# A float32 encoder trunk on one core: where seven-product block pairs stand in the down projection, and in which order their parts are converted and multiplied

## The chip, the cores and the metric

One NeuronCore of a Trainium2 chip runs the whole program. The metric is device time in microseconds (us) of one execution; lower is better. Before the change three runs gave 2872.09, 2876.46 and 2876.27 us, a median of 2876.27 us.

## What is computed

The reference is two layers of a bidirectional encoder over 256 tokens of width 2048, in float32. Only the second half of a layer matters here:

```python
        h2 = rms_norm(x, norm2_g[l])
        u = jax.nn.relu(h2 @ w_up[l])
        x = x + (u * u) @ w_down[l]
```

`w_up` is 2048 x 8192 and `w_down` is 8192 x 2048, so the product `(u * u) @ w_down` has 256 rows, an inner size of 8192 and 2048 columns.

## The kernel before

Every large product is made on TensorE with operands split in two: a block of weights of 128 x 2 x 512 elements comes from memory into a `raw` or `rawx` tile (six of them in the second half of a layer), ScalarE writes its rounded part `hi` (tile `whi`, L208 or L226), and VectorE writes the remainder `lo` (tile `wlo`, L209 or L229). A product is then three matmuls of 512 columns (L244 with `hi`, L245 with `lo`, L246 with `hi` again). The program runs through a list of slots; a plain slot is one such block, four products, 12 matmuls. `run_steps` emits slot i on TensorE and, in the middle of it, calls `ahead(i)`, which emits the conversion of slot i + 3 (`convert`), then the loads that have room (`fetch`, L173) and then the loads of block sums (`fetch_sums`, L200 to L203). There are four pairs of `hi` and `lo` tiles, so the conversion of a slot writes into the tiles of the slot four places earlier and waits until TensorE has finished with them. Each engine takes its instructions strictly in the order in which they were emitted. All DMAs but those of L201 go out from SyncE's queue.

The down projection goes in quarters q of 2048 inner elements. In a quarter, columns are taken 1024 at a time as a pair (`add_pair`): two pairs in each of the first three quarters, one in the last, so 7 pairs in a layer and 14 in the run. A pair has 8 places s along the inner size, 256 elements each. At a plain place there are two plain slots (n = 0 and 1). At the three places of `SEVEN` the 2 x 2 blocks are multiplied with 7 products in place of 8 (a Strassen-Winograd scheme): four slots of kinds a, b, c and d with 2, 2, 2 and 1 products.

- Kind a needs the block b0 alone (an ordinary `raw` tile).
- Kinds b and c need sums of weight blocks, held in tile `tsum` (T, four blocks of 128 x 512). A DMA from SyncE loads two blocks into T[1:3] (L200), a DMA from GpSimd adds two more onto them (L201), and VectorE makes T[0] (L227) and T[3] (L228) by adding the two halves of b0.
- Kind d needs the block b22 alone, loaded by L203.

There are two T tiles, used in turn: the sums of the third place of a pair go into the tile of its first place. `fetch_sums` may load sums for at most two places beyond the number that is `used` up, and the load waits until the conversions that read the tile have ended.

Four PSUM banks hold the results of the pair, and four others (tile `psum`: P[1], P[5], P[6], P[7]) gather four of the seven products over the three places. After the last of these, `middle_down` combines them in pieces and adds them to x (L801 an addition to x, L806 a sum, L810 a copy on ScalarE); each piece is run at the beginning of a plain slot. `after_pair` then adds the result banks to x (four instructions, L834). The next unit's accumulators take the banks in turn.

Of the kernel before, what the change touches and what calls it, by code (L numbers as in the profile page):

```python
# [10 lines left out]
F32 = mybir.dt.float32  # L11
FR = mybir.dt.float32r
BF16 = mybir.dt.bfloat16
ACTF = mybir.ActivationFunctionType
ALU = mybir.AluOpType
# [21 lines left out]
AHEAD = 3  # L37
CONVERT_SLOT = 2
RAW_BUFS = 4
SEVEN = (1, 3, 4)  # L40


def shape_constants():
# [28 lines left out]
def encoder_trunk(ctx: ExitStack, tc: tile.TileContext, I, out: bass.AP):  # L72
    nc = tc.nc
# [39 lines left out]
    def start(gen):  # L113
        lanes.append([gen, 0])
# [26 lines left out]
    def add_raw(w, r, c, mlp=False):  # L141
        raws.append((w[r:r + 256, c:c + BLK], mlp))
        return len(raws) - 1
# [6 lines left out]
    def add_pair(w, r0, c0, nkc, act, sums, half, middle, after):  # L150

        u = {"act": act, "after": after, "n": nkc, "form": "pair", "sums": sums, "half": half, "middle": middle}
        for s in range(nkc // 2):
            if s in SEVEN:
                q = {"r": add_raw(w, r0 + 256 * s, c0, True), "w": w[r0 + 256 * s:r0 + 256 * (s + 1), c0:c0 + 2 * BLK],
                     "i": len(summed)}
                summed.append(q)
                for kind in "abcd":
                    slots.append({"u": u, "s": s, "kind": kind, "q": q})
            else:  # L160
                for n in range(2):
                    slots.append({"u": u, "s": s, "kind": "plain", "n": n,
                                  "raw": add_raw(w, r0 + 256 * s, c0 + n * BLK, True)})

    def fetch():

        while free and st["dma"] < len(raws):
            src, mlp = raws[st["dma"]]
            b = free.pop(0)
            if b is not None and not mlp:  # L170
                continue
            t = raw_p.tile([128, 2, BLK], F32, tag="raw", name="raw") if b is None else b
            nc.sync.dma_start(out=t, in_=src.rearrange("(k p) f -> p k f", p=128))  # L173
            raw_t[st["dma"]] = (t, b)
            st["dma"] += 1

    def take(j):
        t, b = raw_t.pop(j)
        return t, lambda: free.append(b)

    def more_room(c):

        T = one.tile([128, 2, 4, BLK], F32, tag="merged", name="tsum")
        c["SU"] = y_p.tile([128, len(SEVEN), 2, 4, 128], FR, tag="yT", name="SU")
        X = y_p.tile([128, 6, BLK], F32, tag="yT", name="rawx")
# [4 lines left out]
    def fetch_sums():  # L190


        while L.get("T") is not None and st["sum"] < min(st["used"] + 2, len(summed)):
            q = summed[st["sum"]]
            if q["i"] >= L["T_end"]:
                return
            T, q["b22"] = L["T"][q["i"] % 2]
            q["T"] = T
            w = q["w"]
            nc.sync.dma_start(out=T[:, 1:3, :], in_=w[0:128, :].rearrange("p (n f) -> p n f", n=2))  # L200
            nc.gpsimd.dma_start(out=T[:, 1:3, :], in_=w[:, BLK:2 * BLK].rearrange("(k p) f -> p k f", p=128),  # L201
                                accum_op=ALU.add)
            nc.sync.dma_start(out=q["b22"], in_=w[128:256, BLK:2 * BLK])  # L203
            st["sum"] += 1

    def lead(hi, lo, src):

        nc.scalar.activation(out=hi, in_=src, func=ACTF.Copy)  # L208
        nc.vector.tensor_tensor(out=lo, in0=src, in1=hi.bitcast(F32), op=ALU.subtract)  # L209

    def convert(upto):
        while st["cv"] <= min(upto, len(slots) - 1):
            sl = slots[st["cv"]]
            kind = sl["kind"]
            hi = hl_p.tile([128, 2, BLK], FR, tag="hi", name="whi")
            lo = hl_p.tile([128, 2, BLK], FR, tag="lo", name="wlo")
            if kind == "plain":
                r, done = take(sl["raw"])
                lead(hi, lo, r)
                done()  # L220
            else:
                q = sl["q"]
                T = q["T"]
                if kind == "a":
                    b0, done = take(q["r"])
                    nc.scalar.activation(out=hi, in_=b0, func=ACTF.Copy)  # L226
                    nc.vector.tensor_tensor(out=T[:, 0, :], in0=T[:, 2, :], in1=b0[:, 0, :], op=ALU.add)  # L227
                    nc.vector.tensor_tensor(out=T[:, 3, :], in0=T[:, 0, :], in1=b0[:, 1, :], op=ALU.add)  # L228
                    nc.vector.tensor_tensor(out=lo, in0=b0, in1=hi.bitcast(F32), op=ALU.subtract)  # L229
                    done()  # L230
                elif kind == "b":
                    lead(hi, lo, T[:, 0:2, :])
                elif kind == "c":
                    lead(hi, lo, T[:, 2:4, :])
                else:
                    lead(hi[:, 1, :], lo[:, 1, :], q["b22"])
                    st["used"] += 1
            hl_t[st["cv"]] = (hi, lo)
            st["cv"] += 1

    def product(o, a, w, kk, first, last):

        hi, lo = w
        nc.tensor.matmul(o, a[0], hi[:, kk, :], start=first, stop=False)  # L244
        nc.tensor.matmul(o, a[0], lo[:, kk, :], start=False, stop=False)  # L245
        nc.tensor.matmul(o, a[1], hi[:, kk, :], start=False, stop=last)  # L246

    def part(a, kc, t):
        ts = slice(128 * t, 128 * t + 128)
        return a[:, kc, 0, ts], a[:, kc, 1, ts]  # L250
# [14 lines left out]
    def run_steps():  # L265
        held = []
        for i, sl in enumerate(slots):
# [16 lines left out]
            if kind != "plain":  # L284
                seven(u, s, kind, a, w, i)
                continue
# [28 lines left out]
    def ahead(i):  # L315
        convert(min(i + AHEAD, 2 * i + 1))
        fetch()
        fetch_sums()
# [10 lines left out]
    def seven(u, s, kind, a, w, i):  # L329

        ps, k0, k1 = u["ps"], 2 * s, 2 * s + 1
        first, last = s == SEVEN[0], s == SEVEN[-1]
        if "P" not in u:
            p = four_banks(1 - u["half"], "psum")
            u["P"] = {1: p[0][0], 6: p[0][1], 5: p[1][0], 7: p[1][1]}
        P, z = u["P"], u["sums"]()[:, SEVEN.index(s)]
        sums = lambda j: (z[:, 0, j - 1, :], z[:, 1, j - 1, :])
        if kind == "a":  # L340
            product(P[1], part(a, k0, 0), w, 0, first, last)
            ahead(i)
            product(ps[0][0], part(a, k1, 0), w, 1, False, False)
        elif kind == "b":
            product(P[6], sums(2), w, 0, first, last)
            ahead(i)
            product(P[5], sums(1), w, 1, first, last)
        elif kind == "c":
            product(P[7], sums(3), w, 0, first, last)
            ahead(i)  # L350
            product(ps[0][1], part(a, k1, 1), w, 1, False, False)
        else:
            ahead(i)
            product(ps[1][0], sums(4), w, 1, False, False)
            if last:
                start(u["middle"](P))

    def feature_banks(u):

# [407 lines left out]
    def after_up(n):  # L767
        def f(ps):
# [14 lines left out]
            def task():  # L783
                for p in range(2):
                    k0 = 4 * n + 2 * p
                    split((U[:, k0:k0 + 2, 0, :], U[:, k0:k0 + 2, 1, :]), E[p])
                    if k0 // 2 in SEVEN:
                        block_sums(c["SU"][:, SEVEN.index(k0 // 2)], E[p])
                    yield
# [3 lines left out]
    def middle_down(n):  # L793

        def pieces(P):
            c = L["c"]
            rs2 = c["rs2"]

            def add(t, nn, u):
                xs = x[:, t, (n + nn) * BLK:(n + nn + 1) * BLK]  # L800
                nc.vector.scalar_tensor_tensor(out=xs, in0=u, scalar=rs2[:, t:t + 1], in1=xs,  # L801
                                               op0=ALU.mult, op1=ALU.add)

            def plus(tag, a, b, op=ALU.add):
                d = w2_p.tile([128, BLK], F32, tag=tag, name="usum")
                nc.vector.tensor_tensor(out=d, in0=a, in1=b, op=op)  # L806
                return d

            u1 = w2_p.tile([128, BLK], F32, tag="V", name="usum")
            nc.scalar.activation(out=u1, in_=P[1], func=ACTF.Copy)  # L810
            yield
            u2 = plus("V", P[6], u1)
            yield
            add(0, 0, u1)
            u4 = plus("L", P[5], u2, ALU.subtract)
            u3 = plus("L", P[7], u2)
            yield
            u5 = plus("eT", P[5], u3, ALU.subtract)
            yield
            add(0, 1, u4)  # L820
            add(1, 0, u3)
            yield
            add(1, 1, u5)
            c["summed"] = True
        return pieces
# [168 lines left out]
    for l in range(DEPTH):  # L994
# [17 lines left out]
        for q in range(4):  # L1012
# [5 lines left out]
            for n in range(NB if q < 3 else 2, NB):  # L1018
                last = l == DEPTH - 1 and q == 3 and n == NB - 1
# [61 lines left out]
```

## Time and profile before

| | |
|---|---|
| runs, median | 2876.27 us (2872.09 to 2876.46) |
| profiled execution, its own time | 2875.01 us |
| its span in the trace | 2873.2 us |
| TensorE busy | 2844.0 us, 99% |
| VectorE busy | 1799.6 us, 63% |
| ScalarE busy | 1427.5 us, 50% |
| mean granted TensorE clock | 0.998 of 2.4 GHz |

PE is TensorE's matmuls, PEld its weight loads, DVE VectorE, ACT ScalarE, POOL GpSimd, SP SyncE; a q after a name is the engine's queue. In a row of the waits stand the engine, the tile and line that waited, after the arrow what ended the wait, then the sum in us, the number of waits and the longest in us. In a row of the timeline stand the start in us, the duration in us, engine, line, operation, output and inputs, shapes and a count, and in brackets how long the engine was idle just before and what ended that. In a row of one line or tile, durations are minimum/median/maximum in ns. Ends of matmuls are modelled by the profiler; starts are recorded.

### The profile page before, as it was taken

The numbers are of one execution on the slowest core, as the hardware profiler recorded it, in microseconds if no ns is written. First come the engines' busy times: TensorE is split into PE (matmuls) and PEld (weight loads), VectorE is DVE, ScalarE is ACT, GpSimd is POOL, SyncE is SP. The second block draws the span as 40 slices with busy tenths as digits, with TensorE's granted clock in tenths as the row PEclk, the third lists the DMA queues.
The fourth block names the chain that finished last, engine by engine and source line by source line (L and its number), as shares of the span: only waits on it lengthen the run. The fifth ranks groups of instructions, "written<-read, shape, count | busy, mean of one in ns | idle before, by whom it ended". The sixth has DMA issues, their size and how long they took to land.

```text
span 2873.2 us, 36216 instructions
## 1 busy us (share of the span) xinstructions
PE 2844.0 (99%) x13816; PEld 2367.1 (82%) x13816; DVE 1799.6 (63%) x2241; ACT 1427.5 (50%) x1818; POOL 155.3 (5%) x146
## 2 busy tenths in 40 slices
PE   8999999999999999999999999999999999999998
PEld 7888888888888888888788888888888888888887
DVE  5465555555677786877644654545556877868775
ACT  5455445444554554555544554454454555545454
POOL 1000001010000010000000000011000000000001
PEclk9999999999999999999999999999999999999999
DMA  7656566555768586775465566655557775857754
GB/s 233 199 152 192 195 177 172 189 185 183 229 220 247 177 256 205 224 218 191 166 213 183 155 195 195 183 162 188 189 185 236 222 223 190 271 178 227 236 179 161
DMA packets 287903, 573.06 MB, mean 199 GB/s; under 512 B 18196, under 2 KB 18382, under 8 KB 287600
## 3 DMA queue, kind: packets, MB, share of 16 engines
q1 hardware_dynamic: 272016, 534.64, 56.1%
q0 software_dynamic: 15376, 35.30, 7.7%
q8 instruction: 108, 1.77, 0.2%
q10 hardware_dynamic: 336, 0.80, 0.1%
q14 instruction: 67, 0.55, 0.1%
HBM read 568.54 MB, written 2.13 MB: 199 GB/s over the span
## 4 chain that ended last, share of the span: by engine, by line
PE 92%; DMA 4%; DVE 2%; ACT 1%; issue 1%; SPq 0%; POOLq 0%; POOL 0%; DVEq 0%
PE acc L244 20%; PE acc L246 20%; PE acc L245 20%; PE acc L262 17%; PE acc L263 8%; DMA tsum<-in_w_down_dram 4%; PE psum L245 1%; PE psum L246 1%; DVE wlo L209 1%; PE psum L244 1%; PE ob L572 1%; PE scb L540 0%; PE xt L419 0%; PE sca L598 0%; ACT whi L208 0%
## 5 line engine op out<-in xcount | busy, mean ns | idle before, releaser
L209 DVE TENSOR_TENSOR wlo<-raw,whi 128x1024 fp32r<-128x1024 f32 x786 | 971.2, 1241 | 707.6 <-ACT whi L208 702.1
L208 ACT ACTIVATE whi<-raw 128x1024 fp32r<-128x1024 f32 x786 | 826.9, 1057 | 727.1 <-PE acc L246 504.7
L262 PE MATMUL acc<-H,whi 128*128 128x512 f32 x2048 | 724.7, 399 | 0.0
L263 PE MATMUL acc<-H,wlo 128*128 128x256 f32 x2048 | 575.2, 281 | 0.0
L244 PE MATMUL acc<-whi,H 128*128 128x512 f32 x1408 | 564.9, 401 | 0.0
L246 PE MATMUL acc<-whi,H 128*128 128x512 f32 x1408 | 550.2, 391 | 0.0
L245 PE MATMUL acc<-wlo,H 128*128 128x512 f32 x1408 | 549.6, 390 | 0.4 <-DVE wlo L209 0.4
L262 PEld LDWEIGHTS acc<-H,whi 128*128 128x128 f32 x2048 | 384.8, 188 | 96.2 <-DVE x L741 0.6
L263 PEld LDWEIGHTS acc<-H,wlo 128*128 128x128 f32 x2048 | 386.9, 189 | 0.3
L244 PEld LDWEIGHTS acc<-whi,H 128*128 128x128 f32 x1408 | 265.1, 188 | 58.8 <-issue 8.1
L246 PEld LDWEIGHTS acc<-whi,H 128*128 128x128 f32 x1408 | 264.7, 188 | 56.9
L245 PEld LDWEIGHTS acc<-wlo,H 128*128 128x128 f32 x1408 | 265.2, 188 | 52.7 <-DVE wlo L209 1.4
L244 PE MATMUL acc<-whi,U 128*128 128x512 f32 x772 | 301.5, 391 | 2.2 <-ACT junk L429 2.2
L245 PE MATMUL acc<-wlo,U 128*128 128x512 f32 x772 | 300.7, 390 | 0.0
L246 PE MATMUL acc<-whi,U 128*128 128x512 f32 x772 | 300.7, 390 | 0.0
L209 DVE TENSOR_TENSOR wlo<-rawx,whi 128x1024 fp32r<-128x1024 f32 (+1 forms) x164 | 177.2, 1086 | 99.2 <-ACT whi L208 96.7
L208 ACT ACTIVATE whi<-rawx 128x1024 fp32r<-128x1024 f32 (+1 forms) x164 | 155.1, 947 | 155.7 <-PE acc L246 79.6
L244 PEld LDWEIGHTS acc<-whi,U 128*128 128x128 f32 x772 | 144.9, 188 | 33.1 <-ACT junk L429 3.0
L246 PEld LDWEIGHTS acc<-whi,U 128*128 128x128 f32 x772 | 145.0, 188 | 30.4
L245 PEld LDWEIGHTS acc<-wlo,U 128*128 128x128 f32 x772 | 145.1, 188 | 29.6
L208 ACT ACTIVATE whi<-tsum 128x1024 fp32r<-128x1024 f32 x84 | 87.9, 1056 | 59.8 <-DVE tsum L227 25.0
L201 POOL DMA_DIRECT2D tsum<-in_w_down_dram x42 | 50.6, 1206 | 1198.0 <-DMA tsum<-in_w_down_dram 820.0
(193 smaller groups left out, 2763.1 us busy)
## 6 DMA issues: line engine op xcount, KB each, us to landing
raw<-in_w_in_dram SPq DMA_DIRECT2D x352, 512.0 KB, 4.1
raw<-in_w_up_dram SPq DMA_DIRECT2D x180, 512.0 KB, 4.3
raw<-in_w_down_dram SPq DMA_DIRECT2D x154, 512.0 KB, 4.7
rawx<-in_w_up_dram SPq DMA_DIRECT2D x76, 512.0 KB, 4.5
raw<-in_w_out_dram SPq DMA_DIRECT2D x64, 512.0 KB, 4.2
rawx<-in_w_down_dram SPq DMA_DIRECT2D x60, 512.0 KB, 5.2
tsum<-in_w_down_dram SPq DMA_DIRECT2D x42, 512.0 KB, 5.6
tsum<-in_w_down_dram POOLq DMA_DIRECT2D x42, 512.0 KB, 9.5
```

The source lines that it names most:

```text
L201: nc.gpsimd.dma_start(out=T[:, 1:3, :], in_=w[:, BLK:2 * BLK].rearrange("(k p) f -> p k f", p=128), accum_op=ALU.add)
L208: nc.scalar.activation(out=hi, in_=src, func=ACTF.Copy)
L209: nc.vector.tensor_tensor(out=lo, in0=src, in1=hi.bitcast(F32), op=ALU.subtract)
L244: nc.tensor.matmul(o, a[0], hi[:, kk, :], start=first, stop=False)
L245: nc.tensor.matmul(o, a[0], lo[:, kk, :], start=False, stop=False)
L246: nc.tensor.matmul(o, a[1], hi[:, kk, :], start=False, stop=last)
L262: nc.tensor.matmul(ps[j], hi[:, kk, fs], a[:, kc, :, :], start=first, stop=False)
L263: nc.tensor.matmul(ps[j][:, S:2 * S], lo[:, kk, fs], a[:, kc, 0, :], start=False, stop=last)
L572: nc.tensor.matmul(o[:, g, :], eT[:, 2 * g + kc, :], c["vb"][:, kc, col:col + 64], start=kc == 0, stop=kc == 1)
```

## The change

`SEVEN` goes from places 1, 3 and 4 to 1, 3 and 5 (counted from 0), so that two plain slots stand between all places with 7 products. The order of kinds goes from a, b, c, d to a, d, b, c, in the list of slots and so in conversion and multiplication. The two additions that make T[0] and T[3] move from the conversion of a to that of b, behind the conversions of a and d; b0's tile is given back there. The copy of P[1] (first piece of `middle_down`) is emitted in the last slot a of the pair, and the other pieces are packed into four, since four plain slots are left behind the last place.

```diff
-SEVEN = (1, 3, 4)
+SEVEN = (1, 3, 5)
...
-                for kind in "abcd":
+                for kind in "adbc":
...
                 if kind == "a":
                     b0, done = take(q["r"])
-                    nc.scalar.activation(out=hi, in_=b0, func=ACTF.Copy)
+                    lead(hi, lo, b0)
+                    q["b0"], q["done"] = b0, done
+                elif kind == "d":
+                    lead(hi[:, 1, :], lo[:, 1, :], q["b22"])
+                elif kind == "b":
+                    b0 = q["b0"]
                     nc.vector.tensor_tensor(out=T[:, 0, :], in0=T[:, 2, :], in1=b0[:, 0, :], op=ALU.add)
                     nc.vector.tensor_tensor(out=T[:, 3, :], in0=T[:, 0, :], in1=b0[:, 1, :], op=ALU.add)
-                    nc.vector.tensor_tensor(out=lo, in0=b0, in1=hi.bitcast(F32), op=ALU.subtract)
-                    done()
-                elif kind == "b":
+                    q["done"]()
                     lead(hi, lo, T[:, 0:2, :])
-                elif kind == "c":
+                else:
                     lead(hi, lo, T[:, 2:4, :])
-                else:
-                    lead(hi[:, 1, :], lo[:, 1, :], q["b22"])
                     st["used"] += 1
...
             product(ps[0][0], part(a, k1, 0), w, 1, False, False)
+            if last:
+                u["rest"] = u["middle"](P)
+                next(u["rest"])
+        elif kind == "d":
+            ahead(i)
+            product(ps[1][0], sums(4), w, 1, False, False)
...
             if last:
-                start(u["middle"](P))
+                start(u["rest"])
...
             u2 = plus("V", P[6], u1)
-            yield
             add(0, 0, u1)
             u4 = plus("L", P[5], u2, ALU.subtract)
+            yield
+            add(0, 1, u4)
             u3 = plus("L", P[7], u2)
             yield
             u5 = plus("eT", P[5], u3, ALU.subtract)
-            yield
-            add(0, 1, u4)
             add(1, 0, u3)
             yield
             add(1, 1, u5)
```

VectorE's order in the first pair of the run, from the plain place 2 to the last seven-product place, before (`tsum` is T; a `wlo` of 128x1024 from `raw` at L229 is that of kind a, the 128x512 one is that of kind d):

```order
L209 TENSOR_TENSOR wlo<-raw,whi 128x1024 x2
L227 TENSOR_TENSOR tsum<-tsum,raw 128x512
L228 TENSOR_TENSOR tsum<-tsum,raw 128x512
L229 TENSOR_TENSOR wlo<-raw,whi 128x1024
L209 TENSOR_TENSOR wlo<-tsum,whi 128x1024 x2
L209 TENSOR_TENSOR wlo<-rawx,whi 128x512
L227 TENSOR_TENSOR tsum<-tsum,raw 128x512
L228 TENSOR_TENSOR tsum<-tsum,raw 128x512
L229 TENSOR_TENSOR wlo<-raw,whi 128x1024
L209 TENSOR_TENSOR wlo<-tsum,whi 128x1024 x2
L209 TENSOR_TENSOR wlo<-rawx,whi 128x512
```

The same stretch in the changed kernel, where the two additions are L232 and L233:

```order
L209 TENSOR_TENSOR wlo<-raw,whi 128x1024 x3
L209 TENSOR_TENSOR wlo<-rawx,whi 128x512
L232 TENSOR_TENSOR tsum<-tsum,raw 128x512
L233 TENSOR_TENSOR tsum<-tsum,raw 128x512
L209 TENSOR_TENSOR wlo<-tsum,whi 128x1024 x2
L209 TENSOR_TENSOR wlo<-raw,whi 128x1024
L209 TENSOR_TENSOR wlo<-rawx,whi 128x1024 x2
L209 TENSOR_TENSOR wlo<-rawx,whi 128x512
L232 TENSOR_TENSOR tsum<-tsum,rawx 128x512
L233 TENSOR_TENSOR tsum<-tsum,rawx 128x512
L209 TENSOR_TENSOR wlo<-tsum,whi 128x1024 x2
```

Nothing that reads T stands ahead of the remainders of a and d any more, and the conversions of two plain slots lie between the second and the third place.

VectorE's order at the end of the first pair, before, from the first sum of P banks to the last addition of `middle_down` (behind it come the two additions to T and the remainder of the next pair's kind a, and then the four rows of `after_pair`):

```order
L806 TENSOR_TENSOR usum<-psum,usum 128x512
L209 TENSOR_TENSOR wlo<-raw,whi 128x1024
L801 SCALAR_TENSOR_TENSOR x<-usum,rs_5619,x 128x512
L806 TENSOR_TENSOR usum<-psum,usum 128x512 x2
L209 TENSOR_TENSOR wlo<-raw,whi 128x1024
L806 TENSOR_TENSOR usum<-psum,usum 128x512
L209 TENSOR_TENSOR wlo<-rawx,whi 128x1024
L801 SCALAR_TENSOR_TENSOR x<-usum,rs_5619,x 128x512 x2
L209 TENSOR_TENSOR wlo<-rawx,whi 128x1024
L801 SCALAR_TENSOR_TENSOR x<-usum,rs_5619,x 128x512
```

And in the changed kernel, where they are L810 and L805 (behind the last row, the remainder of the next pair's kind a, come the four rows of `after_pair`, L837):

```order
L810 TENSOR_TENSOR usum<-psum,usum 128x512
L805 SCALAR_TENSOR_TENSOR x<-usum,rs_5619,x 128x512
L810 TENSOR_TENSOR usum<-psum,usum 128x512
L209 TENSOR_TENSOR wlo<-raw,whi 128x1024
L805 SCALAR_TENSOR_TENSOR x<-usum,rs_5619,x 128x512
L810 TENSOR_TENSOR usum<-psum,usum 128x512
L209 TENSOR_TENSOR wlo<-rawx,whi 128x1024
L810 TENSOR_TENSOR usum<-psum,usum 128x512
L805 SCALAR_TENSOR_TENSOR x<-usum,rs_5619,x 128x512
L209 TENSOR_TENSOR wlo<-rawx,whi 128x1024
L805 SCALAR_TENSOR_TENSOR x<-usum,rs_5619,x 128x512
L209 TENSOR_TENSOR wlo<-raw,whi 128x1024
```

The same eight instructions lie between fewer conversions: three of them stand ahead of the first.

## Rows read from the trace of the kernel before

**Rows 1.** The page: span, busy time of two engines, granted clock by slice.
```profile
span 2873.2 us, 36216 instructions
PE 2844.0 (99%) x13816; PEld 2367.1 (82%) x13816; DVE 1799.6 (63%) x2241; ACT 1427.5 (50%) x1818; POOL 155.3 (5%) x146
...
PEclk9999999999999999999999999999999999999999
```

**Rows 2.** The waits, of PE alone: two of its five rows.
```profile
PE psum L245 <- DVE wlo L229: 10.5, 9, 1.8
...
PE acc L244 <- ACT junk L429: 2.2, 2, 1.1
```

**Rows 3.** Line 227, the first addition to T: what its engine waited for.
```profile
  DMA tsum<-in_w_down_dram: 18.8, 9
```

**Rows 4.** Timeline of PE where the longest stall stands (third place of a pair).
```profile
1369.90 0.39 PE L244 MATMUL psum<-whi,U 128*128 128x512 f32 x1
1372.10 0.50 PE L245 MATMUL psum<-wlo,U 128*128 128x512 f32 x1 [1.81 <-DVE wlo L229]
1372.44 0.42 PE L246 MATMUL psum<-whi,U 128*128 128x512 f32 x1
```

**Rows 5.** Timeline of the same pair: its first place on PE, load of T.
```profile
1354.94 0.39 PE L244 MATMUL psum<-whi,U 128*128 128x512 f32 x1
...
1355.75 0.34 SPq L200 DMA_DIRECT2D tsum<-in_w_down_dram  x1
...
1359.42 1.21 POOL L201 DMA_DIRECT2D tsum<-in_w_down_dram  x1 [110.53 <-DVE wlo L209]
```

**Rows 6.** Timeline of DVE at that pair's third place: additions to T, remainder of a.
```profile
1369.49 0.69 DVE L227 TENSOR_TENSOR tsum<-tsum,raw 128x512 f32<-128x512 f32 x1 [2.74 <-DMA tsum<-in_w_down_dram]
1370.22 0.69 DVE L228 TENSOR_TENSOR tsum<-tsum,raw 128x512 f32<-128x512 f32 x1
1370.83 1.22 DVE L229 TENSOR_TENSOR wlo<-raw,whi 128x1024 fp32r<-128x1024 f32 x1
1371.96 1.22 DVE L209 TENSOR_TENSOR wlo<-tsum,whi 128x1024 fp32r<-128x1024 f32 x1
```

**Rows 7.** Timelines of DVE and ACT at that pair's first place, beside the up projection's end.
```profile
1351.81 0.69 DVE L379 TENSOR_TENSOR U<-u,U 128x512 fp32r<-128x512 f32 x1
1352.76 1.23 DVE L209 TENSOR_TENSOR wlo<-tsum,whi 128x1024 fp32r<-128x1024 f32 x1 [0.26 <-ACT whi L208]
...
1354.51 1.22 DVE L209 TENSOR_TENSOR wlo<-tsum,whi 128x1024 fp32r<-128x1024 f32 x1
...
1351.68 1.04 ACT L208 ACTIVATE whi<-tsum 128x1024 fp32r<-128x1024 f32 x1
1355.20 0.63 ACT L208 ACTIVATE whi<-rawx 128x512 fp32r<-128x512 f32 x1 [1.00 <-PE acc L246]
```

**Rows 8.** Timelines where that layer's last pair ends: DVE, then PE.
```profile
1393.27 1.23 DVE L209 TENSOR_TENSOR wlo<-raw,whi 128x1024 fp32r<-128x1024 f32 x1 [0.83 <-ACT whi L208]
1394.41 2.72 DVE L834 SCALAR_TENSOR_TENSOR x<-acc,rs,x 128x512 f32<-128x512 f32 x4
...
1391.30 0.39 PE L244 MATMUL acc<-whi,U 128*128 128x512 f32 x1
...
1394.47 0.39 PE L246 MATMUL acc<-whi,U 128*128 128x512 f32 x1
1395.96 0.47 PE L244 MATMUL acc<-whi,U 128*128 128x512 f32 x1 [1.10 <-ACT junk L429]
```

**Rows 9.** Lines 801 and 806: the instructions that combine P banks.
```profile
L801 DVE SCALAR_TENSOR_TENSOR x<-usum,rs,x x56: 742/745/747, 856.1 to 2816.5; 128x512 f32<-128x512 f32 x56
...
L806 DVE TENSOR_TENSOR usum<-psum,usum x56: 678/681/687, 854.1 to 2811.3; 128x512 f32<-128x512 f32 x56
```

**Rows 10.** Lines 201 and 200: T's two DMAs, from issue to landing.
```profile
DMA to landing us min/median/max: 7.6/9.5/12.8
...
DMA to landing us min/median/max: 3.1/5.6/8.3
```

More of the change, by code (lines that the diff above doesn't have):

```diff
@@ L347, in seven @@
             product(P[5], sums(1), w, 1, first, last)
-        elif kind == "c":
+        else:
             product(P[7], sums(3), w, 0, first, last)
@@ L351, in seven @@
             product(ps[0][1], part(a, k1, 1), w, 1, False, False)
-        else:
-            ahead(i)
-            product(ps[1][0], sums(4), w, 1, False, False)
             if last:
-                start(u["middle"](P))
+                start(u["rest"])
     def feature_banks(u):
```

## The prediction

> **What bounds the kernel now.** I read the page first. TensorE is busy for 2844.0 of 2873.2 us and its granted clock stands at 9 tenths or more in all 40 slices [rows 1]. The change neither adds nor removes a matmul, so it can only win or lose time in which TensorE stands still, and that is little: 29 us by the page. The waits of PE say how much of it the change can reach. The largest of five entries lies in the stage that the diff touches: PE waits for the remainder of a kind-a block (L229), 9 times, 10.5 us, the longest 1.8 us [rows 2]. The next question is what holds that remainder. Line 227, an addition to T that stands ahead of it on VectorE, waited for the DMA of `tsum` 9 times, 18.8 us [rows 3]: as many waits as TensorE has, so the root is not VectorE's load but a late transfer.
>
> The timeline of the worst case shows the whole chain. At the third seven-product place TensorE issues its first matmul at 1369.90, and the second, which needs `lo`, only at 1372.10 [rows 4]. VectorE had waited 2.74 us for T and began the additions at 1369.49; `lo` began at 1370.83 and ended at 1372.05 [rows 6]. T is the tile that the first place of this pair used. That place began on TensorE at 1354.94 (call it A); the load of T left at 1355.75, when kind c's remainder, begun at 1354.51, had been read out of it [rows 5, 7]. Load, accumulating DMA and arrival took 1369.49 - 1355.75 = 13.74 us [rows 5, 6].
>
> **What a stall costs.** In steady state matmuls start 0.226 us apart: 1391.30 to 1394.47 is 14 steps [rows 8]. The wait in brackets counts from a modelled end 0.39 us after the start, so each of the 9 waits hides 0.39 - 0.23 = 0.16 us more. The matmul behind the stall is followed after 0.34 us rather than 0.23, another 0.11 [rows 4]. Together 10.5 + 9 x 0.16 + 9 x 0.11 = **12.9 us** that the change could give back.
>
> The Trainium skill, "Perfetto Trace Analysis", Tensor Engine Instruction, says that the profiler estimates a TensorE instruction's end and does not observe it. By that rule busy and idle sums are not to be trusted and starts are; by the idle sum alone the gain would be 10.5 us.
>
> **The change, part by part.**
>
> *T's deadline.* Before, the third place begins at A + 14.96 [rows 4, 5], its second matmul 0.23 later, and additions and remainder take 1372.05 - 1369.49 = 2.56 us plus 0.05 to reach TensorE [rows 4, 6]. So the first addition had to start at A + 12.58, or 1367.52. It started 1.97 us later, which is the stall: 1372.10 - 1369.90 - 0.23 = 1.97. Now two plain slots more lie in between, 24 x 0.226 = 5.43 us, and T is needed for b, which comes after a and d, nine matmuls or 2.04 us. b's second matmul is then at A + 14.96 + 5.43 + 2.04 + 0.23 = A + 22.66. Behind the first addition stand 0.69 of its own, the rounding on ScalarE, 1.04, the remainder, 1.22 [rows 6, 7], and three hand-overs, for which I take 0.3. The first addition must start by A + 19.4.
>
> *T's arrival.* The load leaves when c's remainder is done, and c is now last of four. At the first place of a pair that follows the up projection VectorE still carries that projection's own splits. From its split at 1351.81 [rows 7] the new order gives: d's remainder from 1352.45 (0.69), the second split, the two additions from about 1353.7 to 1355.05, b's rounding from 1354.6 behind the first addition, b's remainder 1355.7 to 1356.9, c's to 1358.05. So L200 leaves at about A + 3.1, 2.3 us later than now. With the same 13.74 us T is there at A + 16.8, **2.6 us ahead of the deadline**. At the pairs that follow a pair the figure is about the same, since there c's rounding waits for the slot in front of the place to end, as kind d's does now (1355.20, A + 0.26) [rows 7], and rounding and remainder follow. All 9 stalls should go: -12.9 us.
>
> *Additions moved from a to b.* They leave a's path and enter b's. b's remainder, at 1356.9, is needed at A + 2.04 + 0.23 = 1357.21, c's, at 1358.05, at 1358.57. Both are covered, by 0.3 and 0.5 us. I cost this at nothing; if VectorE is that much slower, each of the 14 first places pays the excess. b0's tile is given back some 3 us later; it is one of six tiles, and no wait of PE leads to a plain block of w_down, so nothing is charged.
>
> *Kind d earlier.* Same instructions, same queues; its rounding waits for no T. Nothing.
>
> *`middle_down` in four slots.* VectorE has to do four sums (0.68), four additions to x (0.745) [rows 9] and four remainders (1.13 apart [rows 6]) in four plain slots: 10.2 us of work in 48 x 0.226 = 10.87 us. Before, it had six slots. Where the next unit takes other banks, or the remainders run three slots ahead, this is covered. It is not at the last pair of each layer, where the next unit needs the very banks that `after_pair` reads: there TensorE stands 1395.96 - 1394.47 - 0.23 = 1.26 us already [rows 8]. In the old order VectorE was idle 0.83 us ahead of the last remainder [rows 8]; in the new one the remainder ahead of the sums ends about 1.65 us into the four slots (it waits for kind b's tiles), and 10.0 to 10.2 us of work follow, so `after_pair` begins some 11.7 us after 1383.83, the start of the four slots, at 1395.5 where it was 1394.41. That is 1.1 us later, twice: **+2.2 us**, between 0 and 2.6. The copy of P[1] in the last slot a sits on ScalarE between two roundings that both wait for TensorE; nothing.
>
> *Sum.* -12.9 + 2.2 = -10.7 us. The profiled execution took 2875.01 us, so 2864.3; it lies 1.26 us under the median of the runs shown, so I expect **2865.5 us**, 0.37% less.
>
> **The rivals.**
>
> 1. *VectorE becomes the bound at the seams.* From the last place of a pair through the next pair's first, VectorE has hardly a gap: the four slots above, then four `after_pair` additions of 0.7 (2.72 in all [rows 8]), two plain remainders and the work of the first place. My margins for b and c there are 0.3 to 0.6 us. Against it: VectorE is busy for only 1799.6 us of the span [rows 1], and before the change it caught up every time. If each of the 14 pairs pays 0.5 us, 7 of the 10.7 us are lost: 2872.5, no measurable change.
>
> 2. *The load of T gets longer, and the stall comes back larger: slower.* L200 leaves 2.3 us later and so nearer to the loads of plain blocks, and lies on more of the path. Its landing has been as late as 8.3 us and that of L201 12.8 [rows 10]; with 1.2 us to issue [rows 5] that is 22.3 us. From A + 3.1 that would be A + 25.4, a stall of 6.0 us. It decides from 16.3 us on (the deadline less 3.1). At 20 us every pair stalls 3.7 us, 14 x 3.7 = 52 us: 2876.3 + 52 - 10.7, about 2917 us. Against it: where T was waited for it took 13.74 us at its worst stall, and the slow landings are also counted where nobody waited.
>
> The Trainium skill, "DMA: Bandwidth & Descriptors", Issuing engines are not separate DMA queues, says that DMAs of all engines run on the same 16 DMA engines and interleave. It is by that rule that a load moved beside others would be slowed; what it adds here no page states, and the bounds are the landings above.
>
> 3. *The stalls do not come from T alone.* If two plain slots between the places were not what was missing, because kind a's remainder is late for want of its tile, the 9 stalls stay and only the 2.2 us are paid: 2878 us. Against it: the remainder began 0.6 us after the second addition in each step of the timeline, and the additions only when T came [rows 6].
>
> **How the numbers follow.** A run-to-run spread of 2872.09 to 2876.46 us makes 0.2%, or 5.8 us, about the least that a measurement can tell. I give the forecast 0.76, rival 1 0.13, rival 2 0.05, rival 3 0.06. The forecast's own bounds are 2863.4 (nothing paid at the seams) to 2867 (2.6 us paid and 1 us of small stalls). The range runs from 2861, with 2 us of spread below, to 2871, which takes in rival 1 up to 0.4 us a pair. Faster by over 0.2% (under 2870.5): 0.76 + 0.07 of rival 1, 0.83. Within 0.2%: the rest of rival 1 and rival 3, 0.12. Slower: rival 2, 0.05.
>
> **What would show it.** Right: PE has no wait for a remainder of a or b in the pairs; the first addition to T waits for no DMA; T's load leaves some 3 us behind the start of the first place and takes 12 to 14 us; the third place lies 20.4 us behind the first; the gap at the end of a layer's last pair grows from 1.5 to about 2.6 us between starts. Wrong: a wait of PE for b's or c's remainder at first places (rival 1), a wait for `tsum` in line 232 (rival 2), or the same 9 waits at kind a (rival 3).

## The result and the profile after

The changed kernel takes 2861.56 us (median of four runs, 2861.08 to 2862.78); the kernel before, run beside it, 2876.36 us (2872.09 to 2879.57). The ratio is 0.995 with a 95% interval of 0.9933 to 0.9967: 14.8 us less by the medians, where 10.8 were forecast. The profiled executions stand closer together: 2875.01 before, 2862.78 after, 12.2 us less. Part of the difference between the two figures is which run was profiled: before, it lay 1.35 us under its median; after, it was the longest of the four.

The page of the changed kernel, against [rows 1]:

```profile
span 2861.0 us, 36205 instructions
PE 2840.8 (99%) x13816; PEld 2367.1 (83%) x13816; DVE 1792.9 (63%) x2241; ACT 1423.2 (50%) x1818; POOL 155.3 (5%) x146
...
PEclk9999999999999999999999999999999999999999
```

Each of the five counts is the same as before; the 11 fewer instructions in the total are in none of them. The waits of PE, all three that are left, against [rows 2]:

```profile
PE xt L423 <- DMA x<-in_x_dram: 4.1, 2, 2.6
PE acc L245 <- ACT junk L433: 3.9, 2, 2.4
PE v1t L897 <- DMA ident<-in_c_ident_dram: 2.9, 1, 2.9
```

The nine waits for kind a's remainder, 10.5 us, are gone, and no wait for a remainder has come in their place. The two waits at the ends of the layers' last pairs have grown from 2.2 to 3.9 us together.

The pair whose third place stalled longest [rows 4 to 7], in the changed kernel: timelines of PE, SyncE's queue, GpSimd and VectorE. The line numbers of the matmuls are one higher (L245 to L247), the first addition to T is L232.

```profile
1349.95 0.39 PE L245 MATMUL psum<-whi,U 128*128 128x512 f32 x1
...
1352.98 0.34 SPq L200 DMA_DIRECT2D tsum<-in_w_down_dram  x1
...
1358.02 1.21 POOL L201 DMA_DIRECT2D tsum<-in_w_down_dram  x1 [109.07 <-DVE tsum L232]
...
1366.87 0.68 DVE L232 TENSOR_TENSOR tsum<-tsum,rawx 128x512 f32<-128x512 f32 x1
...
1370.35 0.39 PE L245 MATMUL psum<-whi,U 128*128 128x512 f32 x1
1370.58 0.39 PE L246 MATMUL psum<-wlo,U 128*128 128x512 f32 x1
```

With A = 1349.95 the load of T leaves at A + 3.03 (it was A + 0.81), the first addition starts at A + 16.92 without having waited for a DMA (the bracket of L201 names VectorE, but L201 left 0.56 us behind the landing of L200, as it did before the change), and the third place begins at A + 20.40. Its second matmul follows 0.23 us behind the first, where it was 2.20 [rows 4].

What got worse stands at the ends of the layers' last pairs. Timelines of the changed kernel, first the first layer's end (against [rows 8]), VectorE and then PE, then the second's, PE and then ScalarE:

```profile
1384.99 1.21 DVE L209 TENSOR_TENSOR wlo<-raw,whi 128x1024 fp32r<-128x1024 f32 x1
1386.12 2.71 DVE L837 SCALAR_TENSOR_TENSOR x<-acc,rs,x 128x512 f32<-128x512 f32 x4
...
1385.78 0.39 PE L247 MATMUL acc<-whi,U 128*128 128x512 f32 x1
1387.67 0.47 PE L245 MATMUL acc<-whi,U 128*128 128x512 f32 x1 [1.50 <-ACT junk L433]
...
2804.11 0.39 PE L247 MATMUL acc<-whi,U 128*128 128x512 f32 x1
2806.91 0.47 PE L245 MATMUL acc<-whi,U 128*128 128x512 f32 x1 [2.42 <-ACT junk L433]
...
2798.94 1.06 ACT L208 ACTIVATE whi<-raw 128x1024 fp32r<-128x1024 f32 x1 [4.22 <-DMA raw<-in_w_down_dram]
```

The gap between starts was 1.49 us [rows 8]; it is now 1.89 and 2.80 us. At the first layer's end VectorE works through the packed sums without a gap and reaches `after_pair` 0.34 us behind the start of the pair's last matmul; before, it was there 0.06 us ahead. At the second layer's end ScalarE had in addition waited 4.22 us for a plain block (2.04 at the first), and VectorE fell back further.

### The profile page after: what moved, and what is told of

Its sections match the earlier page's. It is cut to its first block, busy times and chain, and to the rows that moved or that the text cites. A ratio compares the mean times of both kernels' runs of the same rounds, so it can differ in the third digit from the quotient of the medians.

```text
span 2861.0 us, 36205 instructions
## 1 busy us (share of the span) xinstructions
PE 2840.8 (99%) x13816; PEld 2367.1 (83%) x13816; DVE 1792.9 (63%) x2241; ACT 1423.2 (50%) x1818; POOL 155.3 (5%) x146
## 4 chain that ended last, share of the span: by engine, by line
PE 98%; DVE 1%; issue 0%; ACT 0%; DMA 0%; POOLq 0%; DVEq 0%; POOL 0%; SPq 0%; ACTq 0%
PE acc L245 22%; PE acc L247 21%; PE acc L246 21%; PE acc L263 17%; PE acc L264 8%; PE psum L247 1%; PE psum L245 1%; PE psum L246 1%; PE ob L576 1%; PE scb L544 0%; PE xt L423 0%; PE sca L602 0%; PE oa L636 0%; PE qkt L493 0%; DVE wlo L209 0%
## 5 line engine op out<-in xcount | busy, mean ns | idle before, releaser
L209 DVE TENSOR_TENSOR wlo<-raw,whi 128x1024 fp32r<-128x1024 f32 x814 | 1001.6, 1239 | 686.5 <-ACT whi L208 683.3
L208 ACT ACTIVATE whi<-raw 128x1024 fp32r<-128x1024 f32 x814 | 852.7, 1057 | 700.5 <-PE acc L247 478.6
L245 PE MATMUL acc<-whi,H 128*128 128x512 f32 x1408 | 564.6, 401 | 0.0
L247 PE MATMUL acc<-whi,H 128*128 128x512 f32 x1408 | 549.9, 391 | 0.0
L245 PEld LDWEIGHTS acc<-whi,H 128*128 128x128 f32 x1408 | 264.9, 188 | 58.9 <-issue 8.1
L247 PEld LDWEIGHTS acc<-whi,H 128*128 128x128 f32 x1408 | 264.6, 188 | 56.5
L245 PE MATMUL acc<-whi,U 128*128 128x512 f32 x772 | 301.9, 391 | 3.9 <-ACT junk L433 3.9
L247 PE MATMUL acc<-whi,U 128*128 128x512 f32 x772 | 301.0, 390 | 0.0
L209 DVE TENSOR_TENSOR wlo<-rawx,whi 128x1024 fp32r<-128x1024 f32 (+1 forms) x178 | 192.1, 1094 | 70.8 <-ACT whi L208 69.9
L208 ACT ACTIVATE whi<-rawx 128x1024 fp32r<-128x1024 f32 (+1 forms) x178 | 168.9, 956 | 122.8 <-PE acc L263 70.0
L245 PEld LDWEIGHTS acc<-whi,U 128*128 128x128 f32 x772 | 145.2, 188 | 34.7 <-ACT junk L433 4.7
L247 PEld LDWEIGHTS acc<-whi,U 128*128 128x128 f32 x772 | 145.3, 188 | 30.4
L209 DVE TENSOR_TENSOR wlo<-tsum,whi 128x1024 fp32r<-128x1024 f32 x84 | 102.2, 1224 | 68.8 <-ACT whi L208 68.8
```

## Experiments

Every run is told beside the kernel before, run on the same chip in the same job: 2872.84 us (nine runs, 2869.41 to 2879.24) for the first four, 2873.70 us (seven runs, 2870.48 to 2876.92) for the last four.

**Place 5 alone.** The change, with the old order and the additions back in a:

```diff
-                for kind in "adbc":
+                for kind in "abcd":
...
                 if kind == "a":
                     b0, done = take(q["r"])
-                    lead(hi, lo, b0)
+                    nc.scalar.activation(out=hi, in_=b0, func=ACTF.Copy)
...
+                    nc.vector.tensor_tensor(out=lo, in0=b0, in1=hi.bitcast(F32), op=ALU.subtract)
```

> The changed kernel with its place 5 and its four pieces of middle_down, but with the old order of kinds (a, b, c, d) and the two additions to T back in the conversion of a. Theory (the stalls came from a late T, and the two plain slots more between second and third place are what mends it): the first addition must start by A + 18.0 (A the start of the first place), T's load leaves at about A + 0.8 as before and T is there at about A + 14.6, so no wait for tsum and no wait of PE for a remainder of kind a; 2861 to 2864 us, like the change. Rival (the order of kinds and the additions behind a are needed too, since VectorE's additions ahead of a's remainder hold it up): PE waits for that remainder at places 3 and 5, some 0.7 us a time, 2868 us or more.

2864.01 us, ratio 0.9968 (0.9955 to 0.9981). No wait for a remainder in the pairs and none for `tsum` on VectorE: the theory's reading holds, and the spacing of places, with the four pieces that go with it, removes the stalls without the new order. It is 2.4 us above the changed kernel's median; the two ratios' intervals overlap, but the trace shows what the order adds. Timeline of PE in this run, at the last place of a pair, from the end of kind a to kind b:

```profile
851.95 0.39 PE L246 MATMUL acc<-whi,U 128*128 128x512 f32 x1
852.35 0.50 PE L244 MATMUL psum<-whi,SU 128*128 128x512 f32 x1
852.68 0.40 PE L245 MATMUL psum<-wlo,SU 128*128 128x512 f32 x1
...
851.70 0.60 ACT L813 ACTIVATE usum<-psum 128x512 f32<-128x512 f32 x1
```

b's first matmul comes 0.40 us behind a's last and the next after 0.33, where 0.23 is the rule: 0.27 us lost, just as ScalarE's copy of P[1] ends (852.30). The same step stands at all 14 last places, 0.28 us each by the starts, 4.0 us together. b writes P[6], which lies in the same tile as P[1].

**The order alone.** Places 1, 3, 4 and six pieces as before, kinds a, d, b, c, additions in b:

```diff
-                for kind in "abcd":
+                for kind in "adbc":
```

> The kernel before with places 1, 3 and 4 and middle_down in six pieces as they were, but with the order a, d, b, c and the additions in the conversion of b. Theory: T's load leaves 2.3 us later than before, since c is now last, and the deadline moves only from A + 12.6 to about A + 14.0, since b comes after a and d; so every third place stalls, by 1.7 to 2.8 us behind the up projection (8 pairs) and up to 0.6 us elsewhere (6 pairs): the stalls cost 18 to 26 us where they cost 13, and stalls over about 2 us bring TensorE's clock down to 1.2 GHz for some matmuls on top, 1 to 2 us each. 2882 to 2900 us. Rival (the additions ahead of a's remainder were the fault): the stalls go and the time is 2863 us.

2887.21 us, ratio 1.004 (1.0025 to 1.0055): slower, as the deadline said. The waits of PE in this run, the first two:

```profile
PE psum L246 <- DVE wlo L209: 10.3, 14, 0.8
PE psum L245 <- ACT whi L208: 7.3, 10, 1.3
```

All 14 pairs now wait for b's parts at the third place, 17.6 us by the modelled ends where 10.5 were lost before; by the starts it is about 24 us where it was 12.9, inside the 18 to 26 expected. The clock falls behind the two longest stalls, which lost 2.5 us each (to 1068.74 and 1204.87). It does not fall behind two that lost 2.4 us (to 2636.47 and 2813.38) and one that lost 2.0, so "over about 2 us" is no limit that this run bears out. The stretch behind one of the two, busy time of each engine, then granted clock, DMA share and GB/s:

```profile
1204.00:1209.00 5.00, 4.24 (x12) 3.27 (x12) 5.00 (x5) 3.94 (x5) 0.64 (x1) 0.66 0.84 195
```

So the half of the change that looks like the cleverer one is a loss by itself: it makes T later by more than it moves the deadline.

**No accumulating DMA.** The kernel before without this instruction:

```diff
-            nc.gpsimd.dma_start(out=T[:, 1:3, :], in_=w[:, BLK:2 * BLK].rearrange("(k p) f -> p k f", p=128),
-                                accum_op=ALU.add)
```

> The kernel before without the 42 accumulating DMAs from GpSimd: T then holds two blocks of weights in place of their sums, so the products of kinds b and c are made from the wrong sums; everything else is as before. Theory: T is ready some 9 us earlier, the nine waits for tsum go and with them TensorE's nine waits for a's remainder: 2861 to 2864 us. Rival (the third place came too soon behind the second for VectorE's and ScalarE's own work): the waits stay, 2873 to 2877 us.

2857.37 us, ratio 0.9939 (0.9924 to 0.9954). VectorE's line for the first addition shows no wait for a DMA at all, and PE's waits for a's remainder are gone, with places, order and pieces as before. So it was T's transfer that held them. This run also takes 42 transfers of 512 KB off the DMA engines and so does not tell T's lateness from the traffic; place 5 alone does, where all DMAs stay. That the time lies 3.6 us under the lower end expected fits the layers' ends, which the old six pieces leave at 1.49 us between starts (1384.39 to 1385.88 in its timeline) where the change pays 1.89 and 2.80 and a fall of the clock behind the second.

**Result banks emptied earlier.** The change, with the first two additions of `after_pair` moved behind the slot that finishes those banks:

```diff
+            if u["form"] == "pair" and s == n // 2 - 1 and sl["n"] == 0:
+                pair_out(ps, 2 * u["half"], 0)
             if final:
...
-                for t in range(2):
-                    nc.vector.scalar_tensor_tensor(out=x[:, t, cols], in0=ps[nn][t], scalar=c["rs2"][:, t:t + 1],
-                                                   in1=x[:, t, cols], op0=ALU.mult, op1=ALU.add)
+                if nn == 1:
+                    pair_out(ps, n, 1)
```

> The changed kernel, with the two additions of after_pair that empty the first two result banks emitted one slot earlier, behind the slot that finishes these banks. Theory (the gaps at the last pair of each layer, 1.9 and 2.8 us between starts in the changed kernel, are VectorE's backlog ahead of these two additions): both gaps fall below 1 us and the clock no longer falls behind the second, 2861.6 - 1.2 - 2.0 - 1.4, about 2857 us. Rival (the gap is set by the last product or by the conversions that wait for raw blocks): 2860 to 2862 us.

2857.80 us, ratio 0.994 (0.9925 to 0.9955). The gap at the first layer's end is gone (another of 1.38 us, in front of transposes of x some 6 us later, gives most of that back: the transposes wait for VectorE); the one at the second is down to 0.77 us, and the clock does not fall behind it. Timeline of PE in this run:

```profile
2804.20 0.39 PE L247 MATMUL acc<-whi,U 128*128 128x512 f32 x1
2804.97 0.47 PE L245 MATMUL acc<-whi,U 128*128 128x512 f32 x1 [0.38 <-ACT junk L435]
```

**final_g loaded later.** The change, with one engine's name exchanged:

```diff
-                nc.gpsimd.dma_start(out=fin["g"], in_=I["final_g"].rearrange("(o d) -> o d", o=1).to_broadcast([128, D]))
+                nc.sync.dma_start(out=fin["g"], in_=I["final_g"].rearrange("(o d) -> o d", o=1).to_broadcast([128, D]))
```

> The changed kernel with the load of final_g (1 MB) issued from SyncE's queue, where it stands behind the last pair's loads, in place of GpSimd's, where it leaves as soon as T is free. Theory (at the last pair of the run that load goes out 1 us ahead of a plain block's and delays it, ScalarE waits 4.2 us for the block, VectorE falls back, and the gap there is 2.8 us where it is 1.9 at the other layer's last pair, long enough for the clock to fall): no wait of ScalarE for raw of w_down over 1 us, a gap of about 1.9 us at both, no matmuls at 1.2 GHz behind it; 2861.6 - 0.9 - 1.4, about 2859.3 us. Rival (the gap there is VectorE's backlog alone): 2861 to 2862 us.

2858.10 us, ratio 0.9944 (0.9929 to 0.9959). ScalarE's longest wait for a block of w_down falls from 4.2 to 1.8 us, not under 1 as I had put it; the gap at the run's last pair falls to that of the other layer, and the clock behind it stays up. Timeline of PE and the stretch behind, in this run:

```profile
2801.62 0.39 PE L247 MATMUL acc<-whi,U 128*128 128x512 f32 x1
2803.51 0.47 PE L245 MATMUL acc<-whi,U 128*128 128x512 f32 x1 [1.50 <-ACT junk L433]
...
2803.00:2809.00 6.00, 5.49 (x24) 4.58 (x25) 3.97 (x5) 4.53 (x10) 0.00 (x0) 1.00 0.84 287
```

**Both.** The two edits together:

```diff
+                pair_out(ps, 2 * u["half"], 0)
...
-                nc.gpsimd.dma_start(out=fin["g"], in_=I["final_g"].rearrange("(o d) -> o d", o=1).to_broadcast([128, D]))
+                nc.sync.dma_start(out=fin["g"], in_=I["final_g"].rearrange("(o d) -> o d", o=1).to_broadcast([128, D]))
```

> The changed kernel with both edits: the first two result banks emptied one slot earlier, and final_g loaded from SyncE's queue. Theory: the gap behind the last pair of the run falls from 0.8 to 0.4 us or less between starts; 2857 to 2858 us, 4 us under the change. Rival (the load of final_g, now later, delays plain blocks of the last two units): 2859 us or more.

2857.02 us (2854.63 to 2859.55), ratio 0.9939 (0.9925 to 0.9954). The wait behind the last pair is gone from PE's list. This is the fastest kernel here by its median, 16.7 us under the kernel before; against the two single edits the difference is inside the spread. Its four runs stand in two groups, 2854.63 and 2854.86 against 2859.17 and 2859.55, with none near the median; the trace is of the shortest and does not show what sets them apart.

**Additions back in a.** The change, with the two additions where they were:

```diff
-                    lead(hi, lo, b0)
-                    q["b0"], q["done"] = b0, done
+                    nc.scalar.activation(out=hi, in_=b0, func=ACTF.Copy)
+                    nc.vector.tensor_tensor(out=T[:, 0, :], in0=T[:, 2, :], in1=b0[:, 0, :], op=ALU.add)
+                    nc.vector.tensor_tensor(out=T[:, 3, :], in0=T[:, 0, :], in1=b0[:, 1, :], op=ALU.add)
+                    nc.vector.tensor_tensor(out=lo, in0=b0, in1=hi.bitcast(F32), op=ALU.subtract)
+                    done()
```

> The changed kernel with the two additions to T back in the conversion of a; places 1, 3, 5 and the order a, d, b, c stay. Theory (with two plain slots between the places T has time to spare, so where the additions stand does not matter): T leaves at about A + 3 and is there at A + 16.8 at the latest, 1.2 us ahead of this order's deadline of A + 18.0; 2861 to 2863 us. Rival (the additions had to move behind a and d): waits of PE for a's remainder, 2866 us or more.

2861.73 us, ratio 0.9955 (0.994 to 0.997), and no wait of PE for a remainder. Where the additions stand makes no difference once the places are two plain slots apart.

**Old order, copy later.** The run with place 5 alone, with the copy of P[1] put behind the last place:

```diff
-            if last:
-                u["rest"] = u["middle"](P)
-                next(u["rest"])
...
-                start(u["rest"])
+                start(u["middle"](P))
...
             nc.scalar.activation(out=u1, in_=P[1], func=ACTF.Copy)
-            yield
```

> The run with place 5 and the old order a, b, c, d, but the copy of P[1] goes back from the last slot a to the first piece behind the place. Theory (what that run lost against the change, some 2.4 us, is a hold of 0.3 us a pair and more at the last b: its product goes into a bank of the tile that ScalarE is just copying P[1] from, and kind d in between hides that copy in the change's order): the step at the last b goes, 2860 to 2862 us, unless the gaps at the layers' ends grow. Rival (the step comes from the roundings of b, late in the order a, b): it stays, 2864 us.

2861.68 us, ratio 0.9954 (0.9938 to 0.9971). The step at the last b is gone at all 14 places; the profiled executions, 2866.12 with the step and 2862.45 without, differ by 3.7 us. Timeline of PE, the same place as above:

```profile
851.27 0.39 PE L246 MATMUL acc<-whi,U 128*128 128x512 f32 x1
851.49 0.39 PE L244 MATMUL psum<-whi,SU 128*128 128x512 f32 x1
851.72 0.39 PE L245 MATMUL psum<-wlo,SU 128*128 128x512 f32 x1
```

So the hold came from the copy. In the change's order kind d stands between a and b, and the step is at none of its 14 places; with the copy put later the old order does as well. Whether the program's ordering by tile or the chip itself makes b wait for the copy, no run here separates.

## Why the prediction was right, and where it was off

- **The wait that counted.** Right. Every stall at the third place went, and the run without the accumulating DMA shows that the late T was behind them.
- **T's deadline and arrival.** The load was put at A + 3.1 and left at A + 3.03, the third place at A + 20.4 and came at A + 20.40: right to 0.1 us. The first addition was put at A + 16.8, with T's arrival as what holds it. It ran at A + 16.92, but that nearness is chance. T's second DMA, issued at 1358.02, had landed at 1366.3, A + 16.4, so T took 13.3 us and not 13.74, and VectorE was then still at the remainders that stand ahead of the addition. L201 in the changed kernel, 1349 to 1371 us, and the timeline of VectorE:

```profile
DMA to landing us min/median/max: 8.3/8.3/8.3
...
1365.14 1.82 DVE L209 TENSOR_TENSOR wlo<-rawx,whi 128x1024 fp32r<-128x1024 f32 x2
```

  The margin to the deadline of A + 19.4 was 3.0 us and not 2.6. The order alone, where the expectation has the same sums put T up to 2.8 us behind its deadline, lost time as they say.
- **What a stall costs.** 12.9 us was the right reckoning for the gaps, but the observation "its granted clock stands at 9 tenths or more in all 40 slices" was read too coarsely. By the starts the nine stalls do sum to 12.9. But behind the 1.97 us stall the kernel before ran some matmuls at 1.2 GHz. Timeline and stretch of the kernel before:

```profile
1373.94 0.63 PE L244 MATMUL psum<-whi,SU 128*128 128x512 f32 x1
1374.37 0.63 PE L245 MATMUL psum<-wlo,SU 128*128 128x512 f32 x1
...
1372.00:1376.00 4.00, 3.90 (x10) 3.10 (x11) 3.65 (x5) 1.94 (x3) 0.00 (x0) 0.58 0.36 131
```

  Eight starts from 1372.67 to 1376.07 take 3.40 us where 8 x 0.226 = 1.81 would do: 1.6 us more that the change gives back. A slice of 72 us shows nothing of that.
- **The seams.** The term of 2.2 us was right in kind and wrong in its parts: +0.40 and +1.31 us, 1.7 together. At the first, VectorE's packed work took 9.6 us (1376.54 to 1386.12), not 10.0 to 10.2. The second seam has a mechanism that I did not name: T is given back at about the same time as the last pair's plain blocks are fetched, and final_g's load, whose tile takes T's place in memory, goes out first. It leaves from GpSimd's queue, so L201 is not the only load that does. Its 1 MB goes out at 2791.56 us, the next plain block at 2792.71; before the change it was 2800.95 and 2805.01. The run with final_g loaded later shows what it cost: 0.91 us of the 1.31. And behind the 2.80 us gap the clock is down in the changed kernel in turn. GpSimd and SyncE's queue in the changed kernel, GpSimd before, then the stretch behind the gap in the changed kernel:

```profile
2791.56 0.59 POOL L864 DMA_DIRECT2D final_g<-in_final_g_dram  x1 [14.64 <-DVE wlo L209]
...
2792.71 1.50 SPq L173 DMA_DIRECT2D raw<-in_w_down_dram  x2
...
2800.95 0.59 POOL L861 DMA_DIRECT2D final_g<-in_final_g_dram  x1 [13.19 <-DVE wlo L209]
...
2808.00:2812.00 4.00, 4.00 (x13) 3.12 (x11) 1.97 (x2) 2.83 (x6) 3.20 (x3) 0.57 0.20 77
```

- **The additions and kind d.** Costed at nothing, and worth nothing by themselves; but I gave the order no gain either, and it has one that I missed, the cover of the copy: the 4.0 us that place 5 alone loses at its last places. "The copy of P[1] in the last slot a ... nothing" holds only because d follows a.
- **The sum.** By the profiled executions: -12.9 for the stalls, -1.6 for the clock behind one of them, +1.7 at the seams and about +1.6 for the clock behind the second, -11.2; measured 12.2. Of what is left, 0.6 is a wait for a remainder in the first 20 us of the program, which the change does not touch: the profiled run of the kernel before has it (18.46 to 19.30 between starts), that of the changed kernel has not. The forecast was 10.7; it had neither fall of the clock, and that the two cancel is luck. The other 2.6 us of the medians' 14.8 come half from each kernel's profiled run, 1.35 us under its median before and 1.22 above it after. The median of 2861.56 us lies under the forecast's own bounds of 2863.4 to 2867, and inside the range only by the 2 us left for spread. The runs of the kernel before spread over 6 to 10 us in each job, the changed kernel's over 1.7 us; that fits a stall that hangs on when a DMA lands, but the single runs have no trace to show it.
- **The rivals.** VectorE as the bound at the seams: only where the next unit takes the same banks. The longer load of T: L201 went out 5.04 us behind L200 in the pair above, 3.67 before [rows 5], since L200 took 4.5 us to land where it had taken 3.1. But L201 then landed in 8.3 us where it had taken 10.1, so the whole was no longer, 13.3 us against 13.7. The stalls that do not come from T: refuted by two runs.

## What to carry to other kernels

When an in-order engine waits for a transfer into a buffer with two copies, write down the time from the last reader of a copy to its next use and hold it against the measured chain of DMAs; spacing the users evenly may cost nothing and is worth more than reordering what happens in between, and a reordering that puts the last reader later can undo it. When work that ran in six slots is packed into four, look for the one seam where the next stage takes the same banks. And see what a buffer that comes free earlier, or just at a busy moment, lets go out ahead of a load that is waited for.

## What was not expected of the hardware

A stall of 2 us of TensorE could be followed by some matmuls at a granted clock of 1.2 GHz (0.425 us between starts in place of 0.226): at 1372.67 in the kernel before, behind a gap of 2.20 us between starts, and in the changed kernel behind the one of 2.80. The length of the gap does not decide it alone. Behind 2.06 us in the kernel before (1019.57 to 1021.63) the clock stayed at 2.4 GHz. With place 5 alone the gaps at the two layers' ends are 2.23 us (1388.86 to 1391.09) and 2.24 us (2808.05 to 2810.29), and the clock fell behind the second only; with the old order and the copy later both are 2.24 us, and it fell behind the first only. The stretches behind the two gaps with place 5 alone, the granted clock third from the end:

```profile
1391.00:1396.00 5.00, 4.91 (x25) 4.09 (x26) 2.88 (x4) 3.69 (x10) 0.00 (x0) 1.00 0.34 124
...
2810.00:2815.00 5.00, 4.71 (x14) 3.77 (x15) 2.98 (x4) 3.46 (x10) 4.58 (x4) 0.66 0.37 115
```

What else decides it, the runs do not show.
